# Input projection of a hybrid encoder layer: from two token chunks to Strassen's seven products in three sweeps

## The chip, the core and the metric

The kernel runs on one core of a Trainium2 chip. The core has a matrix engine (TensorE, PE in the profile; its weight loads are PEld), a vector engine (VectorE, DVE), a scalar engine (ScalarE, ACT), a general one (GpSimd, POOL), a sync engine (SyncE, SP), which issues the transfers here, and 16 DMA engines. Matrix products are written to PSUM, eight banks of 128 x 512 fp32; everything else lives in SBUF or in DRAM. Each engine works through a queue of its own in order, and semaphores tie the queues together. The metric is the device time of one execution in microseconds.

## What is computed

One encoder layer is applied to a prompt of 1024 tokens and to a sample of 256 tokens, each with the same 16 meta tokens ahead, so 1296 different rows, all in fp32:

```python
u = rms_norm(h, norm_w) @ w_in                 # (tokens, 2048) @ (2048, 6656)
qa, ka, va, za, qb, kb, vb, zb = split(u)      # 8, 2, 2, 8, 8, 8, 8, 8 heads of 128
qa, ka = rope(rms_norm(qa)), rope(rms_norm(ka))
ya = global_gqa(qa, ka, va) * silu(za)         # 8 query heads on 2 key heads, all tokens
qb, kb = rms_norm(qb), rms_norm(kb)
yb = neighbourhood_attention(qb, kb, vb, rpb) * silu(zb)   # 8 x 16 window on a grid 64 wide, + meta
return h + concat([ya, yb]) @ w_out            # (tokens, 2048) @ (2048, 2048)
```

## The kernel before

Weights are kept as strips of 128 output columns: 52 strips of `w_in`, 16 of `w_out`, each with 16 k-tiles of 128 contraction rows. To hold fp32 precision every operand of the large products is split into a high part (a cast on ACT, L54) and a low part (a subtraction on DVE, L55), and a product is three matmuls: high times high, low times high, high times low (`strips`, L128 to L130).

The tokens go through in two chunks. `chunk1` holds the 16 meta rows, the 256 sample rows and the first 384 prompt rows; `chunk2` the other 640. Each loads its rows (`get_x`), multiplies them by all 52 strips, and works on the results at once: `qk_evac` (normalisation over the 128 partitions by an all-reduce on POOL, L138, rope, split), `z_evac` (silu), `v_turn` (transposes). Chunk 1 runs the attention of the sample as heads get complete and sends what chunk 2 needs to DRAM. Chunk 2 runs the global attention of the prompt, in blocks of 256 queries (`attend`), the local attention of four heads (`attend_strip`), and projects the other four heads in between (`fill`).

A block of attention computes scores on PE, copies them on ACT, takes the maximum over keys with DVE and one all-reduce on POOL (`all_max`, L202), subtracts on DVE, takes the exponential on ACT, sums on DVE and by a second all-reduce on POOL (`all_sum`, L219), multiplies by the values on PE, and scales and gates the result (`put_y`, L226 to L236, on ACT and DVE). The only work that POOL has, beside setting constants, are these three all-reduces and those of the row norms (L99).

`outproj` runs 16 strips over the first eight heads and then 16 strips over the last eight; the local blocks of the four late heads stand among the first 12 strips (`LSTR`). Both halves work on 512, 512 and 256 columns.

The order on each engine is set by a scheduler from the order of the code and from priorities (`high_priority` draws the weight loads and splits forward); buffers come from pools with fixed numbers of tiles, so that an instruction that needs a tile waits for the last reader of the one it replaces.

Of the kernel before, what the change touches and what calls it, by code (L numbers as in the profile page):

```python
# [22 lines left out]
KT = 16  # L23
NMETA = 16
# [3 lines left out]
C1P = 384  # L28
T1 = NMETA + NS + C1P
T2 = NP - C1P  # L30
# [4 lines left out]
QB = 256  # L35
WIN0 = (0, 1, 3, 4)
WTYPE = (0, 1, 1, 2)
NL = 4
FILL_A = 2
FILL_B = 1  # L40
LSTR = 12
# [3 lines left out]
QA, KA, VA, ZA, QB_, KB, VB, ZB = 0, 8, 10, 12, 20, 28, 36, 44  # L45


class Kern:
# [3 lines left out]
    def split(self, hi, lo, full):  # L52
        nc = self.nc
        nc.scalar.copy(hi, full)  # L54
        nc.vector.tensor_tensor(out=lo, in0=full, in1=hi.bitcast(F32), op=ALU.subtract)  # L55

    def rsqrt(self, ms, n):

        nc = self.nc
        l = self.ev.tile([P, n], F32, tag="ev", name="rs_l")  # L60
        nc.scalar.activation(l[:], ms, AF.Ln)  # L61
        r0 = self.ev.tile([P, n], F32, tag="ev", name="rs_r0")
        nc.scalar.activation(r0[:], l[:], AF.Exp, scale=-0.5)
        nc.scalar.activation(l[:], r0[:], AF.Square, scale=0.5 ** 0.5)
        nc.vector.tensor_tensor(out=l[:], in0=ms, in1=l[:], op=ALU.mult)
        nc.vector.scalar_tensor_tensor(out=r0[:], in0=l[:], scalar=1.5, in1=r0[:], op0=ALU.subtract, op1=ALU.mult)
        return r0

    def start_chunk(self, src, T):

        self.xsrc, self.T, self.xs = src, T, {}
        self.acc = self.xr.tile([P, T], F32, tag="xr", name="xacc")
        self.rb = self.one.tile([P, T], F32, tag="rb", name="rb")
        self.eb = self.one.tile([P, T], F32, tag="eb", name="eb")

    def get_x(self, kt):
        nc = self.nc
        if kt not in self.xs:
            T, acc = self.T, self.acc
            r = self.xr.tile([P, T], F32, tag="xr", name="xr")  # L80
            self.lastx = nc.sync.dma_start(r[:], self.xsrc[:, kt, :]).ins
            h = self.x.tile([P, T], F32R, tag="xh", name="xh")
            l = self.x.tile([P, T], F32R, tag="xl", name="xl")
            w = self.nw[:, kt:kt + 1]
            nc.scalar.activation(h[:], r[:], AF.Copy, scale=w)  # L85
            nc.vector.scalar_tensor_tensor(out=l[:], in0=r[:], scalar=w, in1=h[:].bitcast(F32), op0=ALU.mult, op1=ALU.subtract)  # L86
            if kt == 0:
                nc.scalar.activation(acc[:], r[:], AF.Square, scale=DM ** -0.5)
            else:
                nc.scalar.activation(r[:], r[:], AF.Square, scale=DM ** -0.5)  # L90
                nc.vector.tensor_tensor(out=acc[:], in0=acc[:], in1=r[:], op=ALU.add)
            self.xs[kt] = (h[:], l[:])
            if kt == KT - 1:
                with self.tc.issue_after(self.lastx):
                    for d, c in self.consts:
                        nc.sync.dma_start(d[:], c)
                if self.xsrc is self.io["x1"]:
                    nc.scalar.mul(self.nqkw[:], self.qkw[:], -1.0)
                nc.gpsimd.partition_all_reduce(self.eb[:], acc[:], P, RED.add)  # L99
                nc.vector.tensor_scalar(out=self.eb[:], in0=self.eb[:], scalar1=EPS, scalar2=None, op0=ALU.add)  # L100
                for o in range(0, T, 328):
                    n = min(328, T - o)
                    rr = self.rsqrt(self.eb[:, o:o + n], n)
                    nc.scalar.mul(self.rb[:, o:o + n], rr[:], -1.0)
                nc.vector.tensor_scalar(out=self.eb[:], in0=self.eb[:], scalar1=EPS, scalar2=None, op0=ALU.mult)
        return self.xs[kt]

    def strips(self, jobs, getx):

        nc, tc = self.nc, self.tc  # L110
        out = [[pool.tile([P, 512], F32, tag=tag, name="pp") for pool, tag in pools] for _, _, pools in jobs]
        for c in range(KT // WCH):
            ws = []
            for src, _, _ in jobs:
                with tc.high_priority(offset=self.woff):
                    w = self.raw.tile([P, WCH, P], F32, tag="raw", name="wr")
                    self.lastw = nc.sync.dma_start(w[:], src[:, c * WCH:(c + 1) * WCH, :]).ins
                    wh = self.w.tile([P, WCH, P], F32R, tag="wh", name="wh")
                    wl = self.w.tile([P, WCH, P], F32R, tag="wl", name="wl")
                    self.split(wh[:], wl[:], w[:])  # L120
                    ws.append((wh, wl))
            for k in range(WCH):
                kt = c * WCH + k
                xh, xl = getx(kt)
                for (wh, wl), ps, (_, blocks, _) in zip(ws, out, jobs):
                    for p, (o, n) in zip(ps, blocks):
                        first, last = kt == 0, kt == KT - 1
                        nc.tensor.matmul(p[:, :n], wh[:, k, :], xh[:, o:o + n], start=first, stop=False)  # L128
                        nc.tensor.matmul(p[:, :n], wh[:, k, :], xl[:, o:o + n], start=False, stop=False)  # L129
                        nc.tensor.matmul(p[:, :n], wl[:, k, :], xh[:, o:o + n], start=False, stop=last)  # L130
        return out

    def qk_evac(self, ps, o, n, wc, rope, segs):
        nc = self.nc
        ms = self.ev.tile([P, n], F32, tag="ev", name="ms")
        nc.scalar.activation(ms[:], ps[:, :n], AF.Square, scale=P ** -0.5)  # L136
        m2 = self.ev.tile([P, n], F32, tag="ev", name="m2")
        nc.gpsimd.partition_all_reduce(m2[:], ms[:], P, RED.add)  # L138
        nc.vector.tensor_tensor(out=m2[:], in0=m2[:], in1=self.eb[:, o:o + n], op=ALU.add)  # L139
        if rope is not None:  # L140
            t = self.ev.tile([P, n], F32, tag="ev", name="t")
            nc.scalar.activation(t[:], ps[:, :n], AF.Copy, scale=wc)
            ts = self.ev.tile([P, n], F32, tag="ev", name="ts")
            for i in range(4):
                nc.sync.dma_start(ts[32 * i:32 * i + 32], t[32 * (i ^ 1):32 * (i ^ 1) + 32])
            c, s = rope
            nc.vector.tensor_tensor(out=t[:], in0=t[:], in1=c, op=ALU.mult)
            nc.vector.tensor_tensor(out=ts[:], in0=ts[:], in1=s, op=ALU.mult)
            nc.vector.tensor_tensor(out=t[:], in0=t[:], in1=ts[:], op=ALU.add)
# [5 lines left out]
        for a, m, hi, lo in segs:  # L155
            if lo is None:
                nc.sync.dma_start(hi, r[:, a:a + m])
            else:
                self.split(hi, lo, r[:, a:a + m])
# [742 lines left out]
```

## Time and profile before

| | us |
|---|---|
| median of three runs | 2297.74 (2293.63 to 2299.23) |
| the profiled execution | 2295.91 |
| its span, first to last instruction | 2294.1 |
| PE busy | 2268.6 |
| DVE busy | 1601.9 |
| ACT busy | 1104.6 |
| POOL busy | 530.9 |

Busy times are sums of one engine's instructions without overlaps; the engines run beside each other. A group's line gives the kernel line, the engine, the operation, what it writes and reads, the shape and the count, then busy time and mean duration, then the engine's idle time before it and what ended that. A duration of PE is longer than the distance between two starts. Sequencer instructions (POOLq, SPq) are listed apart and are not counted as busy.

### The profile page before, as it was taken

What the parts mean: (1) busy time and instruction counts of PE and PEld (TensorE: products, weight loads), DVE (VectorE), ACT (ScalarE), POOL (GpSimd) and SP (SyncE); (2) the same over time, 40 slices, a digit from 0 to 9 for tenths busy, and PEclk for the clock granted to TensorE, in tenths of its full rate; (3) what the DMA queues carried; (4) which work ended last, traced back from release to release, by engine and by line L of the source; (5) the groups of instructions that cost most, each with busy time, mean ns of one, the idle gap of its engine ahead of it and who ended that gap; (6) DMA issues with size and microseconds to landing.
All of it is one profiled execution on the core that took longest, in us unless ns stands there. A gap on an engine that the chain in (4) does not pass through costs nothing.

```text
span 2294.1 us, 40464 instructions
## 1 busy us (share of the span) xinstructions
PE 2268.6 (99%) x15166; PEld 2192.9 (96%) x15166; DVE 1601.9 (70%) x3092; ACT 1104.6 (48%) x2400; POOL 530.9 (23%) x275
## 2 busy tenths in 40 slices
PE   7999999999999999999999999999999999999999
PEld 7999999999999999999999999999999888888888
DVE  6876775555555689999998989998777666652221
ACT  6654554444444566676666665665454333320000
POOL 0322232211121124223223314223233222210000
PEclk9999999999999999999999999999999999999999
DMA  6433333333333442222222222224444966657342
GB/s 199 137 111 112 110 105 111 107 106 106 102 108 107 134 153 72 90 86 75 91 93 87 88 81 75 87 84 138 116 133 115 336 214 191 191 182 277 133 136 79
DMA packets 205733, 290.17 MB, mean 126 GB/s; under 512 B 55360, under 2 KB 125408, under 8 KB 203488
## 3 DMA queue, kind: packets, MB, share of 16 engines
q1 hardware_dynamic: 205536, 287.58, 39.5%
q8 instruction: 119, 1.95, 0.4%
q14 instruction: 78, 0.64, 0.1%
HBM read 216.30 MB, written 64.63 MB: 122 GB/s over the span
## 4 chain that ended last, share of the span: by engine, by line
PE 54%; DVE 3%; ACT 1%; POOL 1%; issue 1%; DMA 1%; SPq 0%; DVEq 0%; POOLq 0%
PE pp L130 8%; PE pp L129 8%; PE pp L128 8%; PE pp L754 7%; PE pp L755 7%; PE pp L756 7%; PE po L393 2%; PE po L296 1%; PE po L294 1%; PE po L295 1%; PE sp L254 1%; PE sp L255 1%; PE sp L256 1%; POOL m L138 1%; PE sp L361 1%
## 5 line engine op out<-in xcount | busy, mean ns | idle before, releaser
L128 PE MATMUL pp<-xh,wh 128*128 128x384 f32 (+2 forms) x3328 | 1025.2, 311 | 11.8 <-ACT xh L85 11.6
L129 PE MATMUL pp<-xl,wh 128*128 128x384 f32 (+2 forms) x3328 | 1030.7, 310 | 1.1 <-DVE xl L86 0.8
L130 PE MATMUL pp<-xh,wl 128*128 128x384 f32 (+2 forms) x3328 | 1029.8, 311 | 0.0
L128 PEld LDWEIGHTS pp<-xh,wh 128*128 128x128 f32 x3328 | 624.1, 188 | 13.7 <-ACT xh L85 13.1
L129 PEld LDWEIGHTS pp<-xl,wh 128*128 128x128 f32 x3328 | 625.8, 188 | 3.4 <-DVE xl L86 3.3
L130 PEld LDWEIGHTS pp<-xh,wl 128*128 128x128 f32 x3328 | 625.7, 188 | 0.2
L55 DVE TENSOR_TENSOR wl<-wr,wh 128x512 fp32r<-128x512 f32 x480 | 368.7, 771 | 226.1 <-ACT wh L54 220.8
L54 ACT CAST wh<-wr 128x512 fp32r<-128x512 f32 x480 | 294.7, 617 | 416.2 <-PE pp L129 198.3
L138 POOL PARTITION_ALL_REDUCE m<-ms x104 | 246.4, 2369 | 423.2 <-ACT ms L136 299.9
L754 PE MATMUL pp<-yh,wh 128*128 128x512 f32 (+1 forms) x768 | 274.6, 358 | 2.5 <-DMA yh<-yd 2.5
L755 PE MATMUL pp<-yh,wh 128*128 128x512 f32 (+1 forms) x768 | 275.0, 358 | 0.0
L219 POOL PARTITION_ALL_REDUCE tot<-a x80 | 170.3, 2128 | 450.6 <-DVE a L217 450.5
L756 PE MATMUL pp<-yh,wl 128*128 128x512 f32 (+1 forms) x768 | 274.2, 358 | 0.0
L202 POOL PARTITION_ALL_REDUCE ma<-m x80 | 106.9, 1336 | 583.9 <-DVE m L200 570.2
L754 PEld LDWEIGHTS pp<-yh,wh 128*128 128x128 f32 x768 | 145.7, 190 | 24.0 <-DMA yh<-yd 2.6
L755 PEld LDWEIGHTS pp<-yh,wh 128*128 128x128 f32 x768 | 145.7, 190 | 20.9
L756 PEld LDWEIGHTS pp<-yh,wl 128*128 128x128 f32 x768 | 145.5, 190 | 20.8
L785 DVE TENSOR_TENSOR o<-pp,o 128x512 f32<-128x512 f32 (+1 forms) x48 | 28.5, 602 | 140.3 <-PE pp L756 140.3
L258 ACT COPY S<-sp 128x512 f32<-128x512 f32 x136 | 77.7, 581 | 61.1 <-PE sp L256 37.1
L275 ACT ACTIVATE S<-S 128x512 f32<-128x512 f32 x136 | 84.4, 629 | 30.1 <-DVE S L274 30.0
L61 ACT ACTIVATE rs_l<-m 128x384 f32<-128x384 f32 (+2 forms) x104 | 49.1, 472 | 102.4 <-DVE m L139 102.2
L55 DVE TENSOR_TENSOR pl<-S,ph 128x512 fp32r<-128x512 f32 x136 | 96.0, 719 | 0.0
(186 smaller groups left out, 3235.6 us busy)
## 6 DMA issues: line engine op xcount, KB each, us to landing
wr<-in_w_in SPq DMA_DIRECT2D x416, 256.0 KB, 3.2
yd<-yt SPq DMA_DIRECT2D x160, 128.0 KB, 2.4
yh<-yd SPq DMA_DIRECT2D x16, 1280.0 KB, 17.4
wr<-in_w_out SPq DMA_DIRECT2D x64, 256.0 KB, 4.0
pd<-o SPq DMA_DIRECT2D x16, 640.0 KB, 4.3
o<-pd SPq DMA_DIRECT2D x16, 640.0 KB, 5.0
bt<-in_bt SPq DMA_DIRECT2D x16, 576.0 KB, 5.3
vw<-vn SPq DMA_DIRECT2D x32, 256.0 KB, 3.6
```

Of the source, the lines that this page charges most:

```text
L54: nc.scalar.copy(hi, full)
L55: nc.vector.tensor_tensor(out=lo, in0=full, in1=hi.bitcast(F32), op=ALU.subtract)
L128: nc.tensor.matmul(p[:, :n], wh[:, k, :], xh[:, o:o + n], start=first, stop=False)
L129: nc.tensor.matmul(p[:, :n], wh[:, k, :], xl[:, o:o + n], start=False, stop=False)
L130: nc.tensor.matmul(p[:, :n], wl[:, k, :], xh[:, o:o + n], start=False, stop=last)
L138: nc.gpsimd.partition_all_reduce(m2[:], ms[:], P, RED.add)
L202: nc.gpsimd.partition_all_reduce(ma[:], m1[:], P, RED.max)
L219: nc.gpsimd.partition_all_reduce(tot[:], a1[:], P, RED.add)
L275: nc.scalar.activation(s, s, AF.Exp, scale=SCALE)
L754: nc.tensor.matmul(p[:, :n], wh, yh[:, o:o + n], start=i == 0, stop=False)
L755: nc.tensor.matmul(p[:, :n], wh, yl[:, o:o + n], start=False, stop=False)
L756: nc.tensor.matmul(p[:, :n], wl, yh[:, o:o + n], start=False, stop=i == 7)
```

## The change

The input projection is computed by Strassen's scheme in Winograd's form. The contraction is cut in two halves of 8 k-tiles, the tokens into two halves of 656 columns (16 meta, 256 sample and 384 prompt rows in the first; 640 prompt rows, with 16 zero columns, in the second), and the strips are paired, mostly a global head's with a local head's (`PAIRS`, 26 pairs). For each pair that is a product of 2 x 2 blocks, made with seven block products in place of eight, and fifteen additions of blocks: four on the tokens, four on the weights, seven on the results. A block product is 8 k-tiles by two column groups (320 or 328 columns, one bank each) by three matmuls (`mm`, L211 to L213).

- **Sweep 1** makes two products per pair, from the original first strip and the first token half. They are added in the evacuation (DVE, L254), scaled by the token norm on POOL (L255), and the first product is scaled on POOL too and stored (L257). Beside it `prep` builds the four sums of token blocks on POOL (L144, L168 to L174) and stores three of them and the last block, split, in DRAM.
- **Sweep 2** makes three products per pair from sums of weight blocks. Each pair loads all four weight blocks; the four additions run on POOL (L302 to L305), the split on ACT and DVE, and the two weight blocks of sweep 3 go to DRAM, split. Partial results are stored (`ud`, `vd`).
- **Sweep 3** makes two products per pair from stored weights and stored token blocks. The samples and the global heads' attention run here as their strips get complete (`third`).
- All local attention, 40 blocks, stands among the first 12 strips of the output projection (`local_blocks`).

All q, k, v and z pass through DRAM (`qd`, `kd`, `vt`, `zd`). Work moves from DVE to POOL: the rope products (L403, L404), the last product of z (L455), the low part of the meta probabilities (L484), three products of `put_y` (L500, L501, L504) and the low part of y (L506 by way of L70). Output projection and attention keep their matmuls. The core of the diff (in order: the split, the matmuls of a block product, the evacuation of sweep 1, the weight sums of sweep 2 and its products, the norm and rope of q and k, the meta probabilities, `put_y`, the output loop):

```diff
-    def split(self, hi, lo, full):
+    def split(self, hi, lo, full, eng=None):
         nc.scalar.copy(hi, full)
-        nc.vector.tensor_tensor(out=lo, in0=full, in1=hi.bitcast(F32), op=ALU.subtract)
+        (eng or nc.vector).tensor_tensor(out=lo, in0=full, in1=hi.bitcast(F32), op=ALU.subtract)
...
+    def mm(self, ps, w, x, k, o, first, last):
+        wh, wl = w
+        for b in range(2):
+            p = ps[:, b, o:HB]
+            xh, xl = x[:, 0, b, o:], x[:, 1, b, o:]
+            self.nc.tensor.matmul(p, wh[:, k, :], xh, start=first, stop=False)
+            self.nc.tensor.matmul(p, wh[:, k, :], xl, start=False, stop=False)
+            self.nc.tensor.matmul(p, wl[:, k, :], xh, start=False, stop=last)
...
+            def make(out, o, e):
+                nc.vector.tensor_tensor(out=out, in0=ps[:, :, o:e], in1=p1[:, :, o - f:e - f], op=ALU.add)
+                nc.gpsimd.tensor_tensor(out=out, in0=out, in1=rb[:, :, o:e], op=ALU.mult)
+            self.evac(kind, glob, j, 0, make)
+            nc.gpsimd.tensor_tensor(out=p1[:], in0=p1[:], in1=rb[:, :, f:], op=ALU.mult)
+            nc.sync.dma_start(self.p1d[i][:], p1[:])
...
+                    s = self.w.tile([P, WCH, P], F32, tag="ws", name="ws")
+                    tt = nc.gpsimd.tensor_tensor
+                    tt(out=s[:], in0=a21[:], in1=a22[:], op=add)
+                    tt(out=a21[:], in0=a11[:], in1=a21[:], op=sub)
+                    tt(out=a11[:], in0=s[:], in1=a11[:], op=sub)
+                    tt(out=a12[:], in0=a12[:], in1=a11[:], op=sub)
+                    for t, o in zip((a11, a21, s), out):
+                        o.append(self.wsplit(t))
+                    for j, t in enumerate((a12, a22)):
+                        h = self.w.tile([P, WCH, P], F32R, tag="wg", name="wg")
+                        self.split(h[:], t[:], t[:])
+                        nc.sync.dma_start(self.wd[i][:, c, j, 0], h[:].bitcast(F32))
+                        nc.sync.dma_start(self.wd[i][:, c, j, 1], t[:])
...
+            ps = self.product(ws[0], self.t2, o)
+            nc.vector.tensor_tensor(out=u2[:], in0=ps[:, :, o:HB], in1=u2[:], op=add)
+            ps = self.product(ws[1], t3, o)
...
+            ps = self.product(ws[2], t1, HM)
...
+            nc.gpsimd.partition_all_reduce(m2[:], flat(ms), P, RED.add)
...
+            nc.gpsimd.tensor_tensor(out=ts[:], in0=ts[:], in1=s, op=ALU.mult)
+            nc.gpsimd.tensor_tensor(out=u[:], in0=u[:], in1=c, op=ALU.mult)
...
-        nc.vector.tensor_tensor(out=pm3[32:M3], in0=sm[32:M3], in1=pm3[32:M3].bitcast(F32), op=ALU.subtract)
+        nc.gpsimd.tensor_tensor(out=pm3[32:M3], in0=sm[32:M3], in1=pm3[32:M3].bitcast(F32), op=ALU.subtract)
...
-        nc.vector.tensor_tensor(out=tot[:], in0=tot[:], in1=r[:], op=ALU.mult)
-        nc.vector.scalar_tensor_tensor(out=r[:], in0=tot[:], scalar=2.0, in1=r[:], op0=ALU.subtract, op1=ALU.mult)
+        nc.gpsimd.tensor_tensor(out=tot[:], in0=tot[:], in1=r[:], op=ALU.mult)
+        nc.gpsimd.tensor_tensor(out=z, in0=z, in1=r[:], op=ALU.mult)
         y = self.t.tile([P, QB], F32, tag="t", name="y")
...
+        nc.vector.scalar_tensor_tensor(out=y[:], in0=tot[:], scalar=2.0, in1=po[:], op0=ALU.subtract, op1=ALU.mult)
+        nc.gpsimd.tensor_tensor(out=y[:], in0=y[:], in1=z, op=ALU.mult)
         yt = self.y.tile([P, 2, QB], F32R, tag="y", name="yt")
-        self.split(yt[:, 0, :], yt[:, 1, :], y[:])
+        self.split(yt[:, 0, :], yt[:, 1, :], y[:], nc.gpsimd)
...
-        while done < 4 * NL and done * LSTR < 4 * NL * (c + 1):
-            next(self.late_blocks)
+        while done < 5 * NH and done * LSTR < 5 * NH * (c + 1):
+            next(blocks)
```

How the instructions stand. In the rows below `L... ISA` with tiles behind it is a partition all-reduce of POOL; a row that is only a line and `ISA` is the instruction that the profile lists as MODIFY_POOL_CONFIG. The build puts one in wherever POOL's queue goes over between all-reduces and elementwise work: twice in the kernel before, 381 times in the changed one.

POOL's queue before, in the global attention of the prompt (ma and tot of attention blocks, m of a q strip's evacuation):

```order
L202 ISA ma<-m_14999 128x256
L138 ISA m_15585<-ms 128x384
L219 ISA tot<-a_15020 128x256
L138 ISA m_15599<-ms 128x256
L202 ISA ma<-m_15126 128x256
```

POOL's queue in the changed program at the same place, one block of a global head (Pm of the meta probabilities, tot, z and y of `put_y`, m of a q strip):

```order
L474 ISA
L474 ISA ma<-m_13192 128x256
L394 ISA m_14914<-ms 128x640
L484 ISA
L484 TENSOR_TENSOR Pm<-Sm,Pm 16x256
L491 ISA
L491 ISA tot<-a_13213 128x256
L500 ISA
L500 TENSOR_TENSOR tot<-tot,r 128x256
L501 TENSOR_TENSOR z<-z,r 128x256
L504 TENSOR_TENSOR y<-y,z 128x256
L70 TENSOR_TENSOR yt<-y,yt 128x256
```

Five elementwise operations came in from DVE's queue, and four bare rows with them.

POOL's queue in sweep 2 (m of a local q strip, then the sums of weight blocks of the next pair); before, POOL had nothing to do with weights:

```order
L394 ISA
L394 ISA m_5704<-ms 128x640
L302 ISA
L302 TENSOR_TENSOR ws<-w_5954,w_5956 128x512
L302 TENSOR_TENSOR ws<-w_5989,w_5991 128x512
L303 TENSOR_TENSOR w_5954<-w_5958,w_5954 128x512
```

The evacuation of a q or k strip and the weights of a later pair share the queue.

By part of the changed program, POOL's queue holds:

| | bare rows | all-reduces | elementwise |
|---|---|---|---|
| sweep 1 | 31 (one at the start, as before) | 15 of 640 or 656 columns | 132 (5 of 16 columns) |
| sweep 2 | 25 | 13 of 640 | 208 of 512, 8 of 640 |
| sweep 3 and attention | 325 | 26 of 640 or 656, 160 of 256 | 36 of 640, 400 of 256 |
| before, whole program | 2 | 266 | none |

More of the change, by code (lines that the diff above doesn't have):

```diff
@@ L23 @@
 KT = 16
+KH = 8
 NMETA = 16
@@ L69, in start_chunk, with et @@
[L69 to L74, printed above, removed]
+        nc.scalar.activation(hi, full, AF.Copy, scale=-1.0)
+        nc.vector.scalar_tensor_tensor(out=lo, in0=full, scalar=-1.0, in1=hi.bitcast(F32), op0=ALU.mult, op1=ALU.subtract)
+    def et(self, shape, name, dtype=F32):
+        return self.ev.tile(shape, dtype, tag="ev", name=name)
@@ L87, in get_x, with mat, prep @@
+    def mat(self, i, k):
+        return self.x[i].tile([P, 2, 2, HB], F32R, tag=f"x{k}", name=f"x{i}")
+    def prep(self):
+        nc = self.nc
+        acc = self.one.tile([P, 2 * HB], F32, tag="rb2", name="xacc2")
+        for kt in range(KT):
+            r = self.xr.tile([P, 2 * HB], F32, tag="xr", name="xq")
+            nc.sync.dma_start(r[:], self.io["x2"][:, kt, :])
             if kt == 0:
@@ L106, in get_x @@
-        return self.xs[kt]
-    def strips(self, jobs, getx):
-        nc, tc = self.nc, self.tc
[L111 to L131, printed above, removed]
```

853 lines of the change are left out of this document (466 added, 387 removed).

## The prediction

> **What bounds the kernel now.** I read the page's busy times and slices first, then TensorE's instructions in order of time, then POOL by line and in order of time, then the DMA issues.
>
> ```profile
> span 2294.1 us, 40464 instructions
> PE 2268.6 (99%) x15166; PEld 2192.9 (96%) x15166; DVE 1601.9 (70%) x3092; ACT 1104.6 (48%) x2400; POOL 530.9 (23%) x275
> POOL   0322232211121124223223314223233222210000
> ```
>
> TensorE has work at 99% of the span, so it bounds the kernel, and what the change takes from it can be gained only as far as no other engine becomes the limit. POOL is busy 23%, never above 0.4 of a slice. The profiled execution took 2295.91 us, 1.8 us more than its span and 0.1% under the median of 2297.74; sums below are made against the span.
>
> The price of a matmul is the distance between starts, not its listed time, because they are pipelined. The rows are TensorE in order of time (start, us of the group):
>
> ```profile
> 200.41 0.34 PE L128 MATMUL pp<-xh,wh 128*128 128x384 f32 x1
> ...
> 200.93 0.28 PE L128 MATMUL pp<-xh,wh 128*128 128x256 f32 x1
> ...
> 201.29 0.27 PE L170 MATMUL tp<-ident,vt 128*128 128x128 f32 x1
> ```
>
> Three matmuls of 384 columns take 0.52 us and three of 256 take 0.36: 0.173 and 0.120 each, 0.41 ns a column between. So 320 columns cost 0.147, 328 cost 0.150, and 272 cost 0.127.
>
> ```profile
> L130 PE MATMUL pp<-xh,wl 128*128 128x384 f32 x1664 | 561.0, 337 | 0.0
> L130 PE MATMUL pp<-xh,wl 128*128 128x256 f32 x1344 | 379.3, 282 | 0.0
> L130 PE MATMUL pp<-xh,wl 128*128 128x272 f32 x320 | 92.8, 290 | 0.0
> ```
>
> **What TensorE saves.** Now: 3 x (1664 x 0.173 + 1344 x 0.120 + 320 x 0.127) = 1469 us. Changed: 26 pairs x 7 products x 8 k-tiles x 2 halves x 3 = 8736 matmuls; 2400 have 328 columns (five of the seven products of the ten k and v pairs), the others 320: 360 + 931 = 1291. TensorE saves 178 us; attention and output projection keep their matmuls. If TensorE stayed the bound, the span would be 2294 - 178 = 2116 plus whatever the sweeps' edges leave open.
>
> **What POOL gains.** The changed program gives POOL 784 elementwise instructions (it has none now) among 214 partition all-reduces. Wherever the two kinds alternate stands a bare ISA row, 381 against 2 now; in the profile that is MODIFY_POOL_CONFIG. The rows are POOL in order of time and by line:
>
> ```profile
> masks.py:199 POOLq MODIFY_POOL_CONFIG  x2: 12/12/12, 1.6 to 1.6; - x2
> 0.72 0.20 POOL masks.py:197 MEMSET ident<- 128x128 f32 x1 [0.29 <-POOLq L891]
> 0.86 0.57 POOL L422 MEMSET Pm<- 128x256 f32 x2
> 10.02 0.57 POOL masks.py:199 TENSOR_SCALAR_AFFINE_SELECT ident<-ident 128x128 f32<-128x128 f32 x1 [8.46 <-issue]
> L99 POOLq MODIFY_POOL_CONFIG  x2: 7/7/7, 10.8 to 10.8; - x2
> 49.54 4.06 POOL L99 PARTITION_ALL_REDUCE eb<-xacc  x1 [38.95 <-DVE xacc L91]
> ```
>
> MODIFY_POOL_CONFIG itself is listed at 12 ns, but the AFFINE_SELECT behind it starts at 10.02, 8.4 us after 1.6, and waits for nothing else (its tile was set from 0.72 to 0.92). The second switch, at 10.8, is covered: its all-reduce waits for DVE until 49.54. So one switch has a visible price, 8.4 us, and two switches a program hide what 381 cost.
>
> The Trainium skill, "GPSIMD Engine Reference", section 2.1, says that the first call after loading such a kernel pays about 6 us (5.95 measured) that no profile instruction shows; 8.4 here agrees in kind and is longer. By 5.95 in place of my prices below the sum would be an estimated 4020 us.
>
> The 8.4 us fell while the DMA engines were full (third row: stretch, then busy times; the last two numbers are DMA share and GB/s), and transfers then took longer than usual:
>
> ```profile
> wr<-in_w_in SPq DMA_DIRECT2D x8, 256.0 KB, 4.9
> wr<-in_w_in SPq DMA_DIRECT2D x416, 256.0 KB, 3.2
> 0.00:12.00 12.00, 4.57 (x18) 4.15 (x19) 5.05 (x7) 7.10 (x11) 1.61 (x9) 1.00 0.76 243
> ```
>
> A strip chunk landed in 4.9 us there against a median of 3.2. If a switch is all transfer, it costs 8.4 x 3.2/4.9 = 5.5 us under light traffic; if none of it, 8.4. I take the middle, 7.0, in attention, and 8.4 in sweeps 1 and 2, which move as much (sweep 2: 4.2 MB of weights read and written and about 1.4 MB of sums and results a pair, in 21 us).
>
> Other POOL prices:
>
> ```profile
> L219 POOL PARTITION_ALL_REDUCE tot<-a x80: 1793/1856/3842, 97.4 to 2045.3; - x80
> L202 POOL PARTITION_ALL_REDUCE ma<-m x80: 1063/1172/3377, 92.6 to 2040.0; - x80
> L99 POOL PARTITION_ALL_REDUCE eb<-xacc x2: 4062/4193/4324, 49.5 to 831.8; - x2
> ```
>
> 1.79 and 1.06 us for the sums and maxima of 256 columns, 4.2 for 640 or 656. No elementwise tensor-tensor of POOL is in this trace. Bounds: from DVE's 0.44 to the all-reduce's 1.79 for 256 columns. I take twice the MEMSET row (0.57 for two of 256, so 0.57 for one with two operands), 2.2 ns a column: 1.14 for 512, 1.43 for 640.
>
> **The stages.** Counts are from the changed program's order.
>
> Sweep 1: TensorE needs 26 x 2 x 48 x 0.147 = 367 us. POOL: 30 switches x 8.4 = 252, 15 all-reduces x 4.2 = 63, 127 elementwise x 1.45 = 185: 500 us, and it can hardly begin before the token scale exists, at 16 k-tiles x 18 matmuls x 0.15 = 43 us. One q evacuation holds seven of the nine ev tiles until POOL is through, so TensorE's banks wait with it. 540 us.
>
> Sweep 2: TensorE 26 x 144 x 0.147 = 553; POOL 25 x 8.4 + 208 x 1.14 + 13 x 4.2 + 8 x 1.43 = 513. TensorE sets it. At the edge 10.7 MB of combined tiles and 4.2 MB of weights must land, 61 us at 243 GB/s, of which two or three products (7 us each) cover about 20: 40 us more. 593 us.
>
> Sweep 3 and all attention: the same load at the edge leaves 61 - 28 = 33, say 40 us with the pools reopened. Then POOL's queue per block of 256 queries: maximum, switch, Pm's low part, switch, sum, switch, four operations of put_y, switch. 325 switches x 7.0 = 2275; 26 all-reduces x 4.2 = 109; 80 x (1.06 + 1.79) = 228; 36 x 1.43 = 51; 400 x 0.57 = 228. Inside put_y two turns to other engines stand open:
>
> ```profile
> L236 DVE SCALAR_TENSOR_TENSOR y<-y,r 128x256 f32<-128x256 f32 x80 | 35.8, 448 | 1.1
> L54 ACT CAST yt<-y 128x256 fp32r<-128x256 f32 x80 | 32.3, 404 | 112.4 <-DVE y L236 107.9 <-DMA va<-vd 1.9 <-DMA vw<-vn 1.9
> ```
>
> 0.45 + 0.40 and some semaphores, 1.2 us a block, 96 in all. Sum 2987 us, 35 us a block of which 28 are switches. Does POOL idle besides? Between its maximum and its sum lie 14 us of switches and 0.6 of Pm; DVE and ACT need there
>
> ```profile
> L274 DVE TENSOR_TENSOR S<-S,ma 128x512 f32<-128x512 f32 x136 | 88.5, 706 | 3.0 <-POOL ma L202 2.9
> L275 ACT ACTIVATE S<-S 128x512 f32<-128x512 f32 x136 | 84.4, 629 | 30.1 <-DVE S L274 30.0
> L280 DVE TENSOR_TENSOR acc<-acc,S x64: 671/677/2206, 879.7 to 1565.8; 128x512 f32<-128x512 f32 x64
> ```
>
> 4 x 0.71, one exponential of 0.63 and up to eight more DVE operations of about 0.7: some 9 us, covered. The next block's maximum stands behind y (L503) in DVE's queue and is ready within the switch that follows yt. TensorE's work in this stretch, 2116 - 367 - 553 - 276 = 920 us, lies under it; what is late next is every projection of sweep 3 behind POOL, at no extra cost.
>
> Tail: TensorE's 20 half-strips of output projection after the last local block, 24 x (0.227 + 0.227 + 0.120) = 13.8 each (512 columns: 14 starts in 3.17 us), 276 us, without POOL:
>
> ```profile
> 2199.70 0.39 PE L756 MATMUL pp<-yh,wl 128*128 128x512 f32 x1
> ...
> 2202.87 0.39 PE L755 MATMUL pp<-yh,wh 128*128 128x512 f32 x1
> ```
>
> Sum: 540 + 593 + 40 + 2987 + 276 = 4436, with 2 us around the span about **4440 us**, 1.93 times the time now. With 5.5 us a switch throughout it is 3860, with 8.4 throughout 4890; elementwise work at 1.79 per 256 columns adds up to 490 in attention, at 0.44 it takes 50 off.
>
> **Rivals.**
>
> *The price is paid once.* If the 8.4 us are the start of a program and a later switch costs as little as its 12 ns listing, POOL's sum in attention is 712 us under TensorE's 920, and TensorE stays the bound: 2116 + 40 + 33 = about 2190, faster by 4.6%. For it: the second switch shows nothing. Against: it could show nothing, covered by 38.95 us of waiting. 8%.
>
> *No switch price, but DVE and POOL hinder each other.* Two DVE rows of 512 columns tell: L280 above, both operands in SBUF, reaches 2206 ns, while the one that reads PSUM never does:
>
> ```profile
> L264 DVE TENSOR_TENSOR mx<-mx,sp x64: 665/674/689, 867.6 to 1548.2; 128x512 f32<-128x512 f32 x64
> ```
>
> So the excess is a wait for POOL, not DVE's own. Per global block DVE then has 11 x 0.68 + 5 x 0.44 = 9.7 us of such work, POOL 5.7, the projections between about 8 (160 us of POOL from the sum above and some 95 of DVE, over 32 blocks): 23.4 in turn, against TensorE's 52 x 0.120 + 26 x 14.1/32 = 17.7. 32 x 5.7 = 182 us on the 2190; local blocks come out about even, 9 against (920 - 566)/40 = 8.9. About 2370, slower by 3%. It decides once DVE's and POOL's sum passes TensorE's. 6%. The Trainium skill, "SBUF — State Buffer", section "SBUF: two separate sides", states such an exclusive lock for DVE operations with two SBUF inputs; both rows agree.
>
> *Blocks do not overlap.* S has five tiles and a global block uses four, so the next block's scores (27 x 0.120), copies and maxima, some 6 us, could fall behind instead of under the switch: 80 x 6 = 480, about 4920. Against it: S comes free with pl, well before the sum. 10%.
>
> **Chances.** The forecast 76%, the rivals 8, 6 and 10. Below 2287 or above 2301 us counts as a difference (0.3%). Faster 8%, within 1%, slower 91%. The range 3600 to 5150 goes a little below 5.5 us a switch and holds the third rival; it leaves out the two without a switch price and the edges of the forecast, 2 in 10.
>
> **What would show it.** MODIFY_POOL_CONFIG some 381 times, POOL idle by "issue" 5 to 9 us before its first operation after each, over 2000 us in all; TensorE below 60% busy after sweep 2 and near 100% in the tail; sweep 1 longer than its 367 us of matmuls, sweep 2 near 590. I am wrong if "issue" before POOL's operations sums to under 500 us, or if L500 and L484 start within 1 us of POOL's operation before them.

## The result and the profile after

The changed kernel takes 4616.66 us (median of four runs, 4606.91 to 4624.78) against 2297.19 us of the kernel before on the same chip (2293.63 to 2299.23): 2.010 times the time, 95% interval 2.005 to 2.015. Forecast were 4440 us with a range of 3600 to 5150, so the direction holds and the time lies 4% above the forecast; the profile below shows the forecast mechanism.

The page of the changed kernel, busy times and slices:

```profile
span 4622.9 us, 39874 instructions
PE 2499.1 (54%) x13902; PEld 2342.8 (51%) x13902; DVE 1591.1 (34%) x2261; ACT 1068.4 (23%) x1990; POOL 1374.1 (30%) x1009
PE   6866758888775445656645433334535431111099
POOL 3455544545441323333223222211111112121200
PEclk8878879988887667878777666666766765555599
DMA  5356466666657223324333310123322321110053
```

No engine is the limit by its busy time: TensorE fell from 99% to 54%, VectorE to 34%, and POOL shows 30%. That is how a queue filled with unlisted time looks. Six of the longest waits of the whole execution name it (who waited, for what: us in total, times, longest):

```profile
DVE y L503 <- POOL tot L500: 1026.1, 72, 34.8
PE po L657 <- POOL Pm L484: 709.9, 31, 30.5
POOL tot L500 <- issue: 509.9, 70, 11.0
POOL ma L474 <- issue: 465.5, 73, 8.7
POOL tot L491 <- issue: 443.9, 69, 11.5
POOL yt L70 <- issue: 328.1, 46, 7.7
```

The others wait for POOL, and POOL waits for "issue", for nothing that the profile shows. Before one line, `tot` of `put_y`, the bare rows look like this:

```profile
L500 POOLq MODIFY_POOL_CONFIG  x140: 87/98/98, 1500.7 to 4379.0; - x140
```

The profile lists two such rows of 0.1 us or less for each switch, so these are 70 switches, and 762 rows are the 381. POOL in order of time, one local block (start, us of the operation, idle before it in brackets):

```profile
3603.79 0.71 POOL L70 TENSOR_TENSOR yt<-y,yt 128x256 fp32r<-128x256 f32 x1 [7.25 <-issue]
3604.58 0.71 POOL L484 TENSOR_TENSOR Pm<-Sm,Pm 16x256 fp32r<-16x256 f32 x1
3612.60 1.81 POOL L491 PARTITION_ALL_REDUCE tot<-a  x1 [7.30 <-issue]
3621.51 0.71 POOL L500 TENSOR_TENSOR tot<-tot,r 128x256 f32<-128x256 f32 x1 [7.10 <-issue]
3622.19 0.71 POOL L501 TENSOR_TENSOR z<-z,r 128x256 f32<-128x256 f32 x1
3622.99 0.79 POOL L504 TENSOR_TENSOR y<-y,z 128x256 f32<-128x256 f32 x1
3630.10 1.08 POOL L474 PARTITION_ALL_REDUCE ma<-m  x1 [6.32 <-issue]
3638.20 0.71 POOL L70 TENSOR_TENSOR yt<-y,yt 128x256 fp32r<-128x256 f32 x1 [7.02 <-issue]
```

From one yt to the next pass 34.4 us: 6.5 of operations and 27.7 of four switches. Nearly all of POOL's idle time here lies in switches, though its listed share is 19%. By stage (borders from TensorE's order: end of sweep 1, of sweep 2, of attention; columns as in the prediction's table of stretches):

```profile
0.00:649.00 649.00, 432.77 (x2526) 418.52 (x2526) 319.28 (x321) 225.32 (x351) 302.10 (x158) 0.82 0.52 169
649.00:1392.00 743.00, 615.48 (x3764) 599.73 (x3764) 390.03 (x423) 220.47 (x365) 358.21 (x229) 0.89 0.62 200
1392.00:4390.00 2998.00, 1227.92 (x6460) 1132.83 (x6460) 836.80 (x1444) 606.45 (x1249) 713.81 (x623) 0.67 0.26 80
4390.00:4623.00 233.00, 222.92 (x1152) 191.68 (x1152) 44.96 (x74) 16.14 (x26) 0.00 (x0) 0.98 0.44 153
```

The distances from the first MODIFY_POOL_CONFIG row of each switch to the start of POOL's next operation sum to 205 us for the 31 of sweep 1, 187 for the 25 of sweep 2 and 2193 for the 325 behind them, 2585 in all. With POOL's busy time that fills 78%, 73% and 97% of the three stretches. Some of these distances also hold a wait for data, so the sums are upper bounds, but close ones: POOL is idle for 5 to 9 us before 373 of the 381 operations behind a switch.

### The profile page after: what moved, and what is told of

The parts are those of the page before. It is cut to its first block, busy times and chain, and to the rows that moved or that the text cites. A ratio compares the mean times of both kernels' runs of the same rounds, so it can differ in the third digit from the quotient of the medians.

```text
span 4622.9 us, 39874 instructions
## 1 busy us (share of the span) xinstructions
PE 2499.1 (54%) x13902; PEld 2342.8 (51%) x13902; DVE 1591.1 (34%) x2261; ACT 1068.4 (23%) x1990; POOL 1374.1 (30%) x1009
## 5 line engine op out<-in xcount | busy, mean ns | idle before, releaser
L211 PE MATMUL pp<-x,wh 128*128 128x320 f32 (+1 forms) x2080 | 692.3, 333 | 190.4 <-ACT wh L69 157.0
L213 PE MATMUL pp<-x,wl 128*128 128x320 f32 (+1 forms) x2080 | 687.2, 331 | 70.4 <-DVE wl L70 70.3
L212 PE MATMUL pp<-x,wh 128*128 128x320 f32 (+1 forms) x2080 | 682.4, 328 | 0.3 <-DVE x L112 0.3
L211 PEld LDWEIGHTS pp<-x,wh 128*128 128x128 f32 x2080 | 425.9, 205 | 201.6 <-ACT wh L69 169.4
L213 PEld LDWEIGHTS pp<-x,wl 128*128 128x128 f32 x2080 | 423.8, 204 | 84.0 <-DVE wl L70 83.6
L212 PEld LDWEIGHTS pp<-x,wh 128*128 128x128 f32 x2080 | 426.6, 205 | 0.6 <-DVE x L112 0.6
L211 PE MATMUL pp<-x,w 128*128 128x320 f32 (+1 forms) x832 | 294.3, 354 | 123.6 <-DVE u L360 73.9
L834 PE MATMUL pp<-yh,wo 128*128 128x512 f32 (+1 forms) x768 | 284.0, 370 | 59.6 <-DMA yh<-yd 38.2
L394 POOL PARTITION_ALL_REDUCE m<-ms x52 | 208.3, 4006 | 280.6 <-issue 192.6
L212 PE MATMUL pp<-x,w 128*128 128x320 f32 (+1 forms) x832 | 288.6, 347 | 0.0
L213 PE MATMUL pp<-x,w 128*128 128x320 f32 (+1 forms) x832 | 286.8, 345 | 0.0
L835 PE MATMUL pp<-yh,wo 128*128 128x512 f32 (+1 forms) x768 | 282.0, 367 | 0.0
L836 PE MATMUL pp<-yh,wo 128*128 128x512 f32 (+1 forms) x768 | 281.0, 366 | 0.0
L491 POOL PARTITION_ALL_REDUCE tot<-a x80 | 145.6, 1820 | 451.0 <-issue 443.9
L562 PE MATMUL po<-ph,va 128*128 128x256 f32 x256 | 91.9, 359 | 311.3 <-DVE S L542 216.5
L211 PEld LDWEIGHTS pp<-x,w 128*128 128x128 f32 x832 | 186.1, 224 | 128.2 <-DVE u L360 76.5
L474 POOL PARTITION_ALL_REDUCE ma<-m x80 | 86.7, 1084 | 497.3 <-issue 465.5
L562 PEld LDWEIGHTS po<-ph,va 128*128 128x128 f32 x256 | 63.9, 250 | 319.4 <-ACT ph L69 319.0
L500 POOL TENSOR_TENSOR tot<-tot,r 128x256 f32<-128x256 f32 x80 | 57.3, 716 | 511.7 <-issue 509.9
## 6 DMA issues: line engine op xcount, KB each, us to landing
yh<-yd SPq DMA_DIRECT2D x16, 1280.0 KB, 11.3
```

What stands on the lines that cost most here:

```text
L211: self.nc.tensor.matmul(p, wh[:, k, :], xh, start=first, stop=False)
L212: self.nc.tensor.matmul(p, wh[:, k, :], xl, start=False, stop=False)
L213: self.nc.tensor.matmul(p, wl[:, k, :], xh, start=False, stop=last)
L394: nc.gpsimd.partition_all_reduce(m2[:], flat(ms), P, RED.add)
L474: nc.gpsimd.partition_all_reduce(ma[:], m1[:], P, RED.max)
L491: nc.gpsimd.partition_all_reduce(tot[:], a1[:], P, RED.add)
```

## The experiments

Theories: (a) the switches of POOL cost the time; (b) VectorE and POOL hinder each other over SBUF; (c) Strassen's own passes cost it. Each run is compared with runs of the kernel before on its chip (2295.4 to 2296.6 us).

**All elementwise work back on VectorE.**

```diff
-nc.gpsimd.tensor_tensor(...)      # 784 operations
+nc.vector.tensor_tensor(...)
```

> All 784 elementwise operations of GpSimd go back to VectorE; the matmuls, the passes through DRAM and the sweeps stay. Of the 381 switches two are left, at the program's start.
> (a) The switches cost the time (measured in the changed kernel: 381 of them, 2585 us, median 6.9): TensorE sets the time again, 2116 us of matmuls plus 70 to 300 us of sweep edges, 2190 to 2420 us; VectorE comes to about 2050 us (1591 + 400 x 0.44 + 208 x 0.70 + 140 x 0.85).
> (b) VectorE and GpSimd hinder each other over SBUF: fast too, below 2420 us, since GpSimd then only reduces.
> (c) Strassen's own passes (stored sums, edges, transfers) cost the time: it stays above 3500 us.

Measured: 2641.66 us, ratio 1.150 (1.148 to 1.152). This is called the VectorE form below. Of the 2320 us lost, 1975 come back when both the switches and POOL's elementwise work go; (c) is out as the main cause, while (a) and (b) are not yet told apart. But the time lies 220 us above the range of (a), and this is still a slower kernel than the one before. The page's busy times, and the stretches of sweep 1, sweep 2, sweep 3 with global attention, local attention, tail:

```profile
PE 2255.2 (86%) x13902; PEld 2137.9 (81%) x13902; DVE 1821.8 (69%) x3045; ACT 1068.1 (41%) x1990; POOL 487.0 (18%) x225
0.00:468.00 468.00, 395.20 (x2527) 388.38 (x2528) 354.25 (x458) 228.05 (x353) 68.50 (x22) 0.94 0.73 235
468.00:1082.00 614.00, 574.49 (x3764) 570.92 (x3763) 445.53 (x634) 213.27 (x364) 55.03 (x16) 0.96 0.75 243
1082.00:1943.00 861.00, 702.49 (x4483) 664.31 (x4482) 688.90 (x1144) 464.37 (x892) 240.64 (x107) 0.89 0.58 186
1943.00:2394.00 451.00, 357.04 (x1972) 320.29 (x1970) 283.44 (x726) 143.43 (x350) 120.62 (x80) 0.82 0.62 174
2394.00:2636.00 242.00, 225.96 (x1161) 193.96 (x1161) 49.65 (x86) 19.02 (x33) 2.24 (x2) 0.96 0.43 149
```

TensorE is busy 84%, 94%, 82%, 79% and 93% of these stretches, so it does not set the time throughout; more on that below.

**POOL's elementwise work without a switch.** Sums and maxima over partitions become elementwise operations on POOL, so the two kinds no longer alternate:

```diff
-nc.gpsimd.partition_all_reduce(ma[:], m1[:], P, RED.max)
+nc.gpsimd.tensor_tensor(out=ma[:], in0=m1[:], in1=m1[:], op=ALU.subtract)
-nc.gpsimd.partition_all_reduce(tot[:], a1[:], P, RED.add)
+nc.gpsimd.tensor_tensor(out=tot[:], in0=a1[:], in1=a1[:], op=ALU.add)
+nc.gpsimd.tensor_tensor(out=tot[:], in0=tot[:], in1=a1[:], op=ALU.add)
...    # the norms' all-reduces likewise, two operations each
```

> The elementwise operations stay on GpSimd, and each partition all-reduce is replaced by one elementwise operation (maxima) or two (sums) of the same size on GpSimd; the sums and maxima over partitions are left out, and the exponential's factor and the norm's factor are changed so that numbers stay finite. So no switch is left in the loop, while GpSimd's elementwise work grows to about 1100 operations.
> (a) The switches cost the time: 2200 to 2500 us, GpSimd about 1200 us busy, no idle time by issue.
> (b) VectorE and GpSimd hinder each other: above 4000 us, as the load on both is nearly the same as in the changed kernel.
> (c) Strassen's own passes: above 3500 us.

Measured: 2672.46 us, ratio 1.164 (1.162 to 1.166), with nearly the busy time on POOL of the changed kernel (1374.1 there):

```profile
PE 2266.1 (85%) x13902; PEld 2144.1 (80%) x13902; DVE 1703.6 (64%) x2261; ACT 1078.4 (40%) x1990; POOL 1348.3 (50%) x1143
```

So nearly all of the loss goes although POOL's work stays; the alternation is what costs. This decides against (b): the run is only 31 us above the one without any elementwise work on POOL. As in the run before, the time lies above the range of (a), by 172 us. The hindrance exists all the same. The first subtraction of a local block, two operands in SBUF, in the run before and in this one:

```profile
L649 DVE TENSOR_TENSOR S<-S,ma x32: 412/424/426, 1957.1 to 2394.5; 128x256 f32<-128x256 f32 x32
```

```profile
L652 DVE TENSOR_TENSOR S<-S,ma x32: 927/934/947, 2017.4 to 2429.8; 128x256 f32<-128x256 f32 x32
```

0.42 against 0.93 us. In the changed kernel the same subtraction runs while POOL is in a switch, and takes 0.42 us again; there it is another operation, the maximum beside `put_y` (L645), that is hindered, 0.70 us against 0.28 in the VectorE form. One more part of the expectation failed: "issue" before Pm did not vanish (206.7 us, 56 times). No switch stands there; a semaphore instruction of POOL's queue does, which lasts 3.3 us in the median, so "issue" can also be a wait for another engine that the profile doesn't name.

**Attention's five operations back on VectorE.**

```diff
-nc.gpsimd.tensor_tensor(out=pm3[32:M3], ...)    # and the four of put_y
+nc.vector.tensor_tensor(out=pm3[32:M3], ...)
```

> Only the five elementwise operations per attention block (Pm's low part and four of put_y) go back to VectorE. About 95 switches are left: those of sweeps 1 and 2, and of rope and z in sweep 3.
> (a) The switches: sweeps 1 and 2 as before the edit, about 1435 us; behind them TensorE's 2116 - 367 - 553 = 1196 us set the time, with a few hundred for the 39 or so switches left in sweep 3: 2600 to 2950 us.
> (b) VectorE and GpSimd hinder each other: GpSimd loses 400 of 784 operations, so about half of the loss comes back, near 3400 us.
> (c) Strassen's own passes: above 4000 us.

Measured: 3115.5 us, ratio 1.357 (1.354 to 1.360). 96 switches are left; 285 fewer give 1501 us, 5.3 each. It is 166 us above the range of (a), and 284 below the time of (b). The range of (a) took TensorE's 1196 us for the stretch behind the sweeps, which is 1554 us long in the VectorE form.

**One operation of Pm on POOL in the kernel before.**

```diff
-nc.vector.tensor_tensor(out=pm3[32:M3], in0=sm[32:M3], ...)
+nc.gpsimd.tensor_tensor(out=pm3[32:M3], in0=sm[32:M3], ...)
```

> The kernel before with one operation per attention block (the low part of Pm, 16 x 256) moved from VectorE to GpSimd, where it stands between the block's two all-reduces: 160 switches more, 2 a block, nothing else changed.
> (a) The switches: GpSimd gets 160 x 6.9 + 80 x 0.95 = 1180 us on top of 531, 1711 of 2294 us, so it does not become the bound, but each block gets 14 us longer between its maximum and its sum. Slower by what the projections beside it do not cover: 2320 to 2800 us.
> (b) VectorE and GpSimd hinder each other: no change within 1%, the operation takes 0.7 us and VectorE is relieved.
> (c) Strassen's own passes: no change, as this kernel has none.

Measured: 2885.94 us, ratio 1.257 (1.255 to 1.259): 590 us for moving 80 operations of 0.71 us, one a block, in a kernel without Strassen. That is what (a) says and (b) and (c) rule out, though 86 us above the range of (a). POOL's rows of Pm (two bare rows a switch, so 80 switches into Pm; as many lead out of it), and the waits:

```profile
L212 POOLq MODIFY_POOL_CONFIG  x160: 87/88/88, 100.0 to 2626.1; - x160
L212 POOL TENSOR_TENSOR Pm<-Sm,Pm x80: 714/716/2196, 107.8 to 2633.3; 16x256 fp32r<-16x256 f32 x80
```

```profile
ACT r L226 <- POOL tot L219: 591.2, 73, 14.9
POOL ma L202 <- DVE m L200: 520.4, 71, 31.2
POOL Pm L212 <- issue: 504.3, 67, 10.2
```

The 160 added switches sum to 1072 us, 6.7 each, which with 606 of operations is 58% of the span. POOL is not full here and waits 520 us for the next block's maximum: the price is paid as latency, 13.4 us a block between maximum and sum, of which 7.4 show in the time, so the work beside it covers nearly half.

**Pm's low part alone, and put_y alone, back on VectorE.** Both ask whether the number of switches counts or Pm's place in the chain.

```diff
-nc.gpsimd.tensor_tensor(out=pm3[32:M3], ...)          # first kernel
+nc.vector.tensor_tensor(out=pm3[32:M3], ...)
...
-nc.gpsimd.tensor_tensor(out=tot[:], ...)              # second: tot, z, y, yt
+nc.vector.tensor_tensor(out=tot[:], ...)
```

> The changed kernel with only Pm's low part (80 operations, between a block's maximum and its sum) back on VectorE. In the local blocks the scheduler then puts the next block's maximum between two operations of put_y, so 355 switches remain of 381.
> (a) The number of switches sets the time; the runs so far give 5.2 us net for each one removed (1975 us for 379, 1501 us for 285): 4617 - 26 x 5.2 = 4480, say 4400 to 4560 us.
> (b) The place of Pm in the chain sets it (TensorE waits 710 us for Pm in the changed kernel): 3900 to 4000 us.

> The changed kernel with put_y's four operations (320) back on VectorE while Pm's low part stays on GpSimd between the maximum and the sum. 234 switches remain of 381.
> (a) The number of switches: 4617 - 147 x 5.2 = 3850, say 3700 to 3950 us.
> (b) The place of Pm: it still stands between the two all-reduces, so most of the loss remains, above 4200 us.

Measured: 4468.55 us (ratio 1.947, 1.943 to 1.950) with 355 switches, and 3654.11 us (1.592, 1.589 to 1.595) with 234. The first is 12 us from the count of switches, and far from the 3900 to 4000 of the place; it shows too that taking one operation out of the chain saves little if the scheduler alternates elsewhere. The second fell 46 us below its range: 963 us for 147 switches, 6.6 each. Over the five runs made from the changed kernel a switch removed is worth 5.1 to 6.6 us of the whole time, near its own length of 6.8.

**Why is the kernel without switches slower than the one before?** First, more tiles for attention, and local blocks spread over more output strips:

```diff
-("t", 6), ("y", 1)
+("t", 9), ("y", 1)
...
-LSTR = 12          # second kernel only, second pass loaded after the loop
+LSTR = 16
```

> The kernel with all elementwise work on VectorE (2642 us) with nine small attention tiles (m1, ma, a1, tot, r, y) in place of six, since a block uses six, so that the next block could begin earlier. It asks where the rest of Strassen's gain went: TensorE has some 2116 us of matmuls, and the stretch with attention (from 1125 us on) holds 315 us of the excess.
> (c1) Blocks wait for these tiles: the stretch of the local blocks, 639 us with TensorE busy 482, shrinks by 60 to 140 us: 2500 to 2580 us.
> (c2) VectorE's order and load set it (76% busy there): within 1%, 2615 to 2660 us.

> As the run before, and the 40 local blocks are spread over all 16 half-strips of the first output pass in place of 12; the tiles of the second pass are loaded only behind them.
> (c3) The local blocks have too little of TensorE's other work beside them (12 half-strips of 13.8 us for 40 blocks): four more half-strips fill 55 us of gaps, 30 to 50 us faster than the run before.
> (c2) VectorE's order and load: no gain, and 10 to 20 us lost on the late load of the second pass.

Measured: 2634.04 us (1.149, 1.147 to 1.150) and 2638.67 us (1.150, 1.148 to 1.151). More tiles do not help. What a wider spread of the blocks would bring stays untested, because the second edit did not bring it about: the scheduler still ran the strips as early as it could, and left the last blocks bare. Two stretches of 50 us of the second run (TensorE's busy time stands behind the length):

```profile
2050.00:2100.00 50.00, 50.00 (x300) 44.09 (x300) 31.28 (x78) 16.04 (x38) 13.61 (x8) 1.00 0.73 212
2350.00:2400.00 50.00, 21.29 (x90) 19.70 (x90) 32.25 (x85) 17.10 (x42) 15.14 (x11) 0.54 0.20 52
```

POOL in order of time in the VectorE form shows such bare blocks:

```profile
2264.93 1.10 POOL L474 PARTITION_ALL_REDUCE ma<-m  x1 [3.58 <-DVE m L472]
2269.35 1.79 POOL L491 PARTITION_ALL_REDUCE tot<-a  x1 [3.32 <-DVE a L489]
2274.72 1.10 POOL L474 PARTITION_ALL_REDUCE ma<-m  x1 [3.58 <-DVE m L472]
```

Maximum, sum, next maximum: about 10 us a block, one after the other (40 local blocks fill the 451 us from 1943 to 2394, 11.3 each).

Second, both kernels without attention, to separate the projection:

```diff
     def attend(self, q, zs, keys, meta, vals, vmeta, ydst):
-        ...
+        for i, d in enumerate(ydst):
+            self.nc.sync.dma_start(d, q[:, i, :].bitcast(F32))
```

> The kernel with all elementwise work on VectorE, with the 80 attention blocks left out: each block only stores its q tile in the place of its result. Projection by Strassen, its passes through DRAM, loads for attention and output projection stay. TensorE has 1291 us of projection, 442 of output (32 x 13.8) and some transposes.
> (d1) Strassen's projection is faster by itself, and attention behind it loses the gain: 80 to 180 us below the next run.
> (d2) The sweeps' own stalls take the gain (sweep 1 took 465 in place of 367, sweep 2 617 in place of 553, the edge behind it 43): 1104 + 371 + 442 = 1917 or more, within 50 us of the next run or above it.

> The kernel before with the 80 attention blocks left out in the same way. TensorE has 1469 us of projection and 442 of output.
> (d1) and (d2) alike: 1911 us plus a start and an end of up to 60 us. Then attention costs the kernel before 2296 less this, and the VectorE form of Strassen's kernel 2642 less the run before; if the second is larger by 250 us or more, attention's place behind the sweeps is what loses most.

Measured: 2105.49 us with Strassen's projection and 1979.15 without, as (d2) said. The projection by itself, meant to save 178 us, loses 126; and attention costs 2641.66 - 2105.49 = 536 us beside Strassen's projection, 2296.6 - 1979.15 = 317 beside the old one, 219 more. The 126 and the 219 make the 345 us by which the VectorE form is slower; attention's part is the larger, if less than the 250 us of the expectation. Strassen's kernel without attention first (DMA packets, then sweep 1, sweep 2, sweep 3, output), then the kernel before without attention:

```profile
DMA packets 364588, 533.37 MB, mean 254 GB/s; under 512 B 120064, under 2 KB 205472, under 8 KB 362400
0.00:459.00 459.00, 391.10 (x2527) 384.48 (x2527) 351.95 (x457) 227.85 (x352) 73.52 (x22) 0.94 0.72 239
459.00:1045.00 586.00, 566.86 (x3764) 565.64 (x3764) 446.56 (x634) 214.17 (x364) 55.27 (x17) 0.98 0.75 256
1045.00:1609.00 564.00, 421.47 (x2547) 413.35 (x2545) 177.39 (x230) 164.49 (x246) 103.25 (x26) 0.85 0.90 290
1609.00:2103.00 494.00, 454.88 (x2315) 385.60 (x2315) 98.83 (x165) 40.12 (x70) 0.00 (x0) 0.96 0.71 223
```

```profile
PE 1946.1 (98%) x12414; PEld 1874.1 (95%) x12414; DVE 912.0 (46%) x1532; ACT 697.7 (35%) x1440; POOL 236.2 (12%) x115
DMA packets 205686, 289.60 MB, mean 146 GB/s; under 512 B 55360, under 2 KB 125408, under 8 KB 203488
```

Against TensorE's 367, 553, 371 and 442 us the four stretches hold 92, 33, 193 and 52 us too much, with 1.8 times the traffic; the old projection keeps TensorE at 98%. Not all of it is waiting: in sweep 3 TensorE is busy 421 us, 50 more than its 371, at a granted clock of 0.85. Most is lost in that sweep. Its waits (TensorE for VectorE's evacuations of its banks, and VectorE for the transfers of rope's operand and of stored partial results):

```profile
PE pp L211 <- DVE u L360: 100.0, 16, 15.0
DVE ts L403 <- DMA ts<-u: 82.9, 8, 18.9
DVE u L360 <- DMA st<-vd: 39.7, 1, 39.7
```

So late transfers can hold VectorE's queue, and with it TensorE's banks. Two candidates, the number of banks and the transfers, were tried:

```diff
-self.three = False; es_q.close()      # first kernel: the third pair of banks stays for sweep 3
...
-        self.nc.sync.dma_start(k[:, ...], self.kd[g][...])     # second: no loads of k, v, z
```

> The run without attention blocks in its VectorE form (2105 us), with the third pair of PSUM banks kept open in sweep 3 too (the banks of attention are not needed there). Its sweep 3 took 564 us for 371 us of matmuls, and TensorE waited 100 us for evacuations there, with the DMA engines 90% busy.
> (f1) The number of banks holds sweep 3: 60 to 110 us faster, 1995 to 2045 us.
> (f2) Transfers hold it (290 GB/s in that stretch): within 30 us, 2075 to 2115 us.

> The run without attention blocks in its VectorE form (2105 us), with the loads of k, v and z for attention left out as well (nothing reads them there); the q tiles are still loaded and stored.
> (f1) The number of banks: sweep 3 stays near 564 us, 2080 to 2110 us.
> (f2) Transfers hold sweep 3: less traffic beside it gives back a good part of its 193 us of excess, 1960 to 2050 us.

Measured: 2074.22 us and 2029.63 us. Sweep 3 in the one and in the other:

```profile
1045.00:1575.00 530.00, 408.84 (x2542) 402.25 (x2542) 191.52 (x233) 163.29 (x249) 103.70 (x26) 0.88 0.95 311
```

```profile
1045.00:1550.00 505.00, 402.24 (x2518) 394.62 (x2516) 173.29 (x224) 155.15 (x220) 100.04 (x29) 0.91 0.81 261
```

Each gives a part: 31 us by the banks (half of the least that (f1) said, from two executions 14 us apart; the DMA engines then run at 95%), 76 by 38 MB less traffic, within the range of (f2), 59 of them in sweep 3. With the loads, ACT's copies of loaded keys went too, so the 76 are not transfers alone. Transfers are the larger part; with either, more than 100 us of the excess of sweep 3 is left, and no run separates its causes. No run shows a form of Strassen's projection that beats the old one: if both gains added up, an estimate of 2105 - 31 - 76 = 1998 us, it would still lie above 1979.

## Why the prediction was right, and where its sum was off

**Switches.** Right in kind, number and nearly in size. 381 were forecast and are there; forecast at 252 + 210 + 2275 = 2737 us, they took 2585. The local block above has the four switches that the prediction gave a block: 35 us, 28 of it switches, against 34.4 and 27.7. Their order is another. Before 63 of the 80 Pm operations no all-reduce stands, so no switch does, and they start within 1 us of the operation before them. The prediction had named such a start of L500 and L484 as a sign of being wrong. For L484 it came and says nothing, because nothing alternates there; L500 has its switch in 70 of 80 cases.

The price was tied to the load on the DMA engines, 5.5 to 8.4 us. That is right in direction and too strong. Means are 6.85 us in sweep 1 (DMA share 0.52; without the one at the start, which took 0.1), 7.48 in sweep 2 (0.62) and 6.75 behind them (0.26), against 8.4, 8.4 and 7.0. The direction of the switch, which the prediction did not consider, matters more: the median is 5.9 to 6.2 us into an all-reduce (L491, L474, L394) and 7.0 to 7.2 into elementwise work (L484, L70, L403, L500). Within one direction the load shows, taking the DMA share during each switch and only those whose idle time is all "issue": into an all-reduce 5.88 us below a share of 0.3 (55 switches) and 6.28 above 0.6 (62); into Pm, in the run that moves Pm alone, 7.27 (33) and 8.08 (12). The load was never varied alone, so its part is not shown to be a cause. That 7.0 came close to 6.75 is partly luck: it was the middle of two bounds on the load, and the average mixes two directions.

The Trainium skill, "GPSIMD Engine Reference", section 2.1, has about 6 us (5.95 measured) for the first call to a freshly loaded kernel of POOL; the way into the all-reduce agrees, the other is 1.1 us longer.

**POOL's elementwise prices.** Too low: 0.57, 1.14 and 1.43 us for 256, 512 and 640 columns were taken from MEMSET; 0.72 to 0.95, 1.3 to 1.6 and 1.6 to 2.2 were measured (means by line; 0.95 is Pm's, on 16 partitions). POOL's elementwise rows sum to about 923 us in place of 712.

**Stages.** Sweep 1: 649 for 540. POOL's 302 + 205 = 507 us agree with the forecast 500 by luck, because switches cost 205 in place of 252 and elementwise work 243 in place of 185. The sum held only this work from 43 us on; the other 99 us are POOL's waits for other engines and transfers, which it put at nothing. Sweep 2: 743 for 593, the largest miss. "TensorE sets it" failed: neither TensorE (615 busy, 62 more than its 553, at a granted clock of 0.89) nor POOL (358 + 187) was full. Each waited in its turn: POOL for weight loads and TensorE for the split weights, with POOL's sums between the two:

```profile
POOL ws L302 <- DMA w<-in_w_in: 137.5, 20, 15.8
```

```profile
PE pp L211 <- ACT wh L69: 99.8, 20, 14.5
```

In the VectorE form sweep 2 took 614 us, and 673 with the work on POOL but no switches; so 70 to 129 us of the 743 hang on the switches. Edge, sweep 3 and attention: 2998 for 3027, where cheaper switches offset dearer operations. Tail: 233 for 276, because 1152 matmuls, 16 half-strips, were left and not 20. The misses, +109, +150, -29 and -43, make the 187 us between 4436 and the span.

**Rivals.** "The price is paid once" is refuted by 380 of 381. "No switch price, but DVE and POOL hinder each other" is refuted as the cause; the two runs that differ in it lie 31 us apart, a net figure, as VectorE also loses work there (1822 to 1704 us busy). The exclusive lock that the Trainium skill states in "SBUF — State Buffer", section "SBUF: two separate sides", agrees with 0.42 against 0.93 us. "Blocks do not overlap" fails in the changed kernel: POOL fills 97% of that stretch, so nothing is lost between blocks. In the VectorE form, where no switches cover it, the last local blocks do follow one after the other. Both switch-free times of the prediction, 2190 and 2370, were too low: they took TensorE's 2116 us as nearly reachable, and 2642 and 2672 were measured. The step that fails there is "if TensorE stayed the bound": the projection by itself costs 126 us in place of saving 178, and attention behind it 536 in place of 317.

**Signs promised.** "Issue" before POOL's operations sums to 2254 us (over 2000 forecast); TensorE is at 41% from 1392 to 4390 (below 60%) and at 96% in the tail; sweep 1 is longer than its 367 us. "Sweep 2 near 590" failed, and of the signs against, that of L484 came without its meaning, as said above.

## What to carry to other kernels

Before moving elementwise work to an engine that also runs all-reduces, count how often its queue changes between the two kinds, in the order that the scheduler makes: here each change cost about 7 us that no busy time shows, and one operation of 0.7 us a block, moved to the wrong place, cost 590 us in 80 blocks. An engine at 30% busy can be the bound; look at "issue" before its operations and at who waits for it. And a saving in matmuls counts only while TensorE stays fed: the block products were to save 178 us by the count of matmuls, and without any switch the kernel still took 345 us more than before.

## What the runs showed of the hardware beyond that

- A switch depends on its direction, 5.9 to 6.2 us into an all-reduce and 7.0 to 7.2 into elementwise work, and somewhat on the traffic beside it (5.88 against 6.28, 7.27 against 8.08).
- The row at masks.py:199, the first of each program, cost 8.4 us in the kernel before and 0.1 in the changed one, so not each such row costs. In the fourteen profiles it took 0.1 us in the three programs whose last operation on POOL is elementwise, and 7.9 to 9.2 in the eleven that end on an all-reduce. That POOL starts with what the execution before left in place would explain it; no run tests that.
- A tensor-tensor of POOL takes as long on 16 partitions as on 128 (Pm 16x256: 0.715 us median; tot 128x256: 0.713).
- A VectorE subtraction of 256 columns took 0.42 us beside an idle POOL and 0.93 beside an elementwise POOL, and the two runs are 31 us apart in 2672.
- The granted clock of TensorE went with its load: 0.82, 0.89, 0.67 and 0.98 in the four stretches of the changed kernel, in which it was busy 67%, 83%, 41% and 96%. The same matmuls of sweep 2 kept it busy 615 us at 0.89 and 567 at 0.98 in the VectorE form without attention. Whether the clock fell because of the stalls is not shown.
